# One expert with a fixed place, the others by their count, a ring in address order, and one branch around the rest

## The chip, the cores and the metric

The kernel runs on one core of a Trainium2 chip, in one launch. The metric is device time in microseconds (us), the median of three runs, and lower is better. The engines are PE (matrix multiply; PEld is its weight load), DVE (vector), ACT (scalar), POOL (GpSimd) and SP, which here issues weight loads. Each engine runs its own list of instructions in order; what one needs from another it waits for at a semaphore.

## The reference

Two transformer blocks run after each other on 512 tokens of width 1024, in float32. The change touches the last part alone, a mixture of experts: each token goes to 4 of 32 experts, and their results are added with gates. Cut to that:

```python
N_EXPERTS, TOP_K, D_MODEL, D_FF_EXPERT = 32, 4, 1024, 1024

def clamped_swiglu(hh):
    x_glu = jnp.minimum(hh[..., ::2], 7.0)
    x_lin = jnp.clip(hh[..., 1::2], -7.0, 7.0)
    return x_glu * jax.nn.sigmoid(1.702 * x_glu) * (x_lin + 1.0)

def moe_ffn(h, router_w, router_b, w1, b1, w2, b2):
    ht = h.reshape(t, d)                               # 512 x 1024
    logits = (ht @ router_w + router_b).astype(jnp.float32)
    top_val, top_idx = lax.top_k(logits, TOP_K)
    gates = jax.nn.softmax(top_val, axis=-1)
    ...                                                # tokens are sorted by expert, in blocks
    u = clamped_swiglu(h_pad[idx] @ w1[e] + b1[e])     # w1[e]: 1024 x 2048
    return u @ w2[e] + b2[e]                           # w2[e]: 1024 x 1024
    ...                                                # y[token] += gate * result

x = layer_norm(DEEPNORM_ALPHA * x + (1.0 + gt2) * ffn, ln2_g, ln2_b)
```

How many tokens an expert gets is known only once the router has run. Worked out with the reference on its own inputs, expert 1 gets 115 tokens, expert 0 gets 44, the next ones by size get 89, 87, 83 and 78; 15 of the experts 1 to 31 get more than 64 tokens, the other 16 get 64 or fewer.

## The kernel before

**Expert stage (`experts`).** The program has a fixed list of 32 places, j = 0 to 31. A place holds 2, 3 or 4 blocks of 32 tokens (`BLOCKS[j]`), so 64, 96 or 128 tokens. Places 0 and 1 belong to experts 0 and 1, with 3 blocks each. Which expert stands at each other place is found at run time: `places_of` counts the tokens of each expert, ranks the experts by count, and writes `order`, from which SP reads the expert's number (line 2140). Experts 0 and 1 are kept ahead by a constant that is added to their key (2 to the 20th). Of the others, ranks 2 and 3 get 4 blocks, ranks 4 to 17 get 3, ranks 18 to 31 get 2; `PLACES` puts a light one and a heavy one in turn, with the two of 4 blocks at j = 8 and 17. All blocks together: 84.

**One place.** `gather` (POOL, an indirect DMA from `hd`) fetches its token rows, `turned` transposes them on PE. `up` multiplies by w1 in 8 units of 128 rows (1 MB each), `swiglu` (DVE and ACT) makes u, `turn_u` transposes it, `down` multiplies by w2 in 4 units of 1 MB. Results are scaled by the gate (ACT) and added into the DRAM tensor `yd` by indirect DMAs from POOL (line 2310), one per block. On PE, `down` of a place stands behind `up` of the next; `slots` works out row numbers for two later places at a time.

**Weights.** Each unit is loaded by SP (`load`, line 1778) into a ring of `RING` = 13 buffers of 1 MB (tag `raw`); a load waits until PE has read what the buffer held 13 loads earlier. `tail` issues the first 13 loads ahead of the stage (`t.pre`): the 8 w1 units of expert 0 and 5 of expert 1. `up` takes from `pre`, `down` issues its own loads.

**The rest.** Tokens for which an expert's place has no room are dealt with after the 32 places. `rest` works out by how many tokens each expert is over, and the largest of these. If it is over 0 (line 2177), `make_lists` writes lists of those tokens, and a loop over all 32 experts (line 2179) runs four branches (line 2182), one for each 128 tokens, each around a copy of `more`: gather, up and down for one block list. Every pass of this loop begins with all engines meeting.

**The end (`final`).** SP loads `yd` in four parts (line 2358); DVE, ACT and POOL add, normalise and store tile by tile. It stands after the branch of line 2177.

Of the kernel before, what the change touches and what calls it, by code (L numbers as in the profile page):

```python
# [17 lines left out]
P = 128  # L18
S = 512
NT = S // P  # L20
NI = 2 * NT
D = 1024
KD = D // P
# [4 lines left out]
E = 32  # L28
TOPK = 4
LIMIT = 7.0  # L30
RING = 13


HEAVY, LIGHT = list(range(2, 18)), list(range(18, E))
PLACES = [0, 1] + [r for pair in zip(LIGHT, HEAVY[2:]) for r in pair]
PLACES[8:8], PLACES[17:17] = [2], [3]
BLOCKS = [4 if 2 <= r < 4 else 3 if r < 18 else 2 for r in PLACES]
LEVELS = (64, 32, 16, 8)
SWIGLU = 1.702

# [20 lines left out]
def constants():  # L61
    i = np.arange(P)
    c = {}
    c["ident"] = np.eye(P, dtype=np.float32)
    t, u = i[:, None], i[None, :]

    pairs = lambda s: ((t // s % 2 == 0) & (u // s == t // s + 1)).astype(np.float32)

    half = lambda m, s, j: m.reshape(P, 64 // s, 2, s)[:, :, j].reshape(P, 64)
    gm = [half(pairs(s), s, 1) for s in LEVELS]  # L70
    gm.append(((t // LEVELS[-1] == u // LEVELS[-1]) & (t <= u)).astype(np.float32))
    c["gmask"] = np.concatenate(gm, 1)
    bd = np.zeros((P, 256), np.float32)
    for h in range(4):
        bd[h * 32:(h + 1) * 32, h * 64:(h + 1) * 64] = 1.0
    c["bdiag"] = bd
    mm = np.zeros((P, 3, P), np.float32)
    mm[:, 0] = t <= u
    mm[:, 1] = t < u
    mm[:, 2] = t <= u  # L80
    c["mmask"] = mm
    xy = np.zeros((P, 4, 64), np.float32)
    for n, sz in enumerate((16, 32)):
        xy[:, 2 * n + 1] = half(pairs(sz), sz, 1)
        xy[:, 2 * n] = half(pairs(sz).T, sz, 0)
    c["xymask"] = xy
    c["dblk"] = np.ascontiguousarray((t // 16 == np.arange(8)[None, :]).astype(np.float32))
    c["eye16"] = np.broadcast_to(np.eye(16, dtype=np.float32).reshape(1, 256), (P, 256)).copy()
    tri = np.zeros((P, S), np.float32)
    tri[:, S - P:] = np.where(u <= t, 0.0, NEG)  # L90
    c["tri"] = tri
    hs = np.zeros((P, 2), np.float32)
    hs[:64, 0] = 1.0
    hs[64:, 1] = 1.0
    c["hsel"] = hs
    c["bd2"] = np.kron(np.eye(2), np.ones((64, 64))).astype(np.float32)

    e = np.arange(E)
    c["places"] = np.broadcast_to(np.stack([np.array(PLACES), 32 * np.array(BLOCKS), np.where(e < 2, 2.0 ** 20, 0) - e]),
                                  (P, 3, E)).astype(np.float32)  # L100
    c["group"] = (i[:, None] // 32).astype(np.float32)
    c["invf"] = np.broadcast_to((10000.0 ** (-np.arange(0, 32, 2, dtype=np.float64) / 32)).astype(np.float32), (P, 16)).copy()
    return c
# [1642 lines left out]
class Tail:  # L1746
# [27 lines left out]

    def load(self, part):

        w = self.k.t(self.k.rawp, [P, self.k.usize], tag="raw")
        self.k.nc.sync.dma_start(w if len(part.shape) == 2 else w.rearrange("p (h n) -> p h n", h=2), part)
        return w

# [340 lines left out]
    def experts(self, ctx):  # L2121
        k = self.k
        nc, I, tc = k.nc, k.I, k.tc
        self.prev = None
        self.mw = mw = k.pool("moew", 2, None, ctx, "right")
        xg = [k.t(mw, [P, D], tag="xg") for _ in range(2)]
        for x in xg:
            nc.gpsimd.memset(x, 0.0)
        xg = self.gather(self.idx[:, 0:1])
        self.biases(ctx)  # L2130
        x = self.turned(xg)
        self.slots(mw, [1])
        xg = self.gather(self.idx[:, 1:2])
        self.places_of(self.late)
        before = None
        for j in range(E):
            if j < 2:
                e, takes = j, k.ident[0:E, j:j + 1]
            else:
                e = nc.values_load(self.order[0:1, j:j + 1], engines=[mybir.EngineType.SP], min_val=0, max_val=E - 1)  # L2140
                takes = self.takes[:, j:j + 1]
            nxt = SimpleNamespace(nb=BLOCKS[j], rows=self.rows[:, j], gate=self.gate[:, j])
            one, nxt.two = self.weight(e)
            then = {}
            if j % 2 == 0 and j + 2 < E:
                then[0] = lambda: self.slots(mw, [j + 2, j + 3])
            if before is not None and before.uT is None:
                then[2] = lambda: self.turn_u(before)
            if j + 1 < E:
                def following():  # L2150
                    nonlocal x, xg
                    x = self.turned(xg)
                    if j + 2 < E:
                        xg = self.gather(self.idx[:, j + 2:j + 3])
                then[4] = following
            self.up(nxt, x, takes, one, then)
            if before is not None:
                self.down(before)
            if j == 0:
                self.turn_u(nxt)  # L2160
                self.down(nxt)
                nxt = None
            before = nxt
            with tc.issue_after(self.behind):
                if j in (2, 10):
                    self.last_rows(j // 8)
                if j == E - 1:
                    self.final_rows()
            if j in LB:
                with tc.issue_after(self.behind):  # L2170
                    self.last_bias(*divmod(LB.index(j), NT))
        self.turn_u(before)
        self.down(before)

        self.rest(self.late)
        most = nc.values_load(self.over[0:1, E:E + 1], min_val=0, max_val=S)
        with tc.If(most > 0):
            self.make_lists(mw)
            with tc.For_i(0, E, 1) as e:  # L2179
                n = nc.values_load(self.over[0:1, bass.ds(e, 1)], min_val=0, max_val=S)  # L2180
                for blk in range(NT):
                    with tc.If(n > P * blk):
                        self.more(e, blk)

    def more(self, e, blk):

# [101 lines left out]
    def down(self, st):  # L2288

        k = self.k  # L2290
        nc, tc = k.nc, k.tc
        mm = nc.tensor.matmul
        ps = [k.t(self.yp, [P, S], tag="y") for _ in range((st.nb + 1) // 2)]
        of = lambda b: ps[b // 2][:, b % 2 * 256:(b % 2 + 1) * 256]
        with tc.issue_after(self.prev):
            for c in range(4):
                w = self.load(st.two(c)).rearrange("p (h n) -> p h n", h=2)
                for h in range(2):
                    for b in range(st.nb):
                        for n in range(4):  # L2300
                            last = mm(of(b)[n * 32:(n + 1) * 32], st.uT[b][:, h, c * 32:(c + 1) * 32], w[:, h, n * 256:(n + 1) * 256],  # L2301
                                      start=c + h == 0 and b % 2 == 0,
                                      stop=c == 3 and h == 1 and (b % 2 == 1 or b == st.nb - 1))
        self.prev = last.ins
        yd = self.yd.rearrange("t (n c) -> (t n) c", n=4)
        done = []
        for b in range(st.nb):
            y = k.t(self.mw, [P, 256], tag="y", bufs=4)
            nc.scalar.activation(y, of(b), AF.Copy, scale=st.gate[:, b:b + 1])  # L2309
            s = nc.gpsimd.indirect_dma_start(out=yd, out_offset=bass.IndirectOffsetOnAxis(ap=st.rows[:, b:b + 1], axis=0),  # L2310
                                             in_=y, in_offset=None, bounds_check=4 * S - 1, oob_is_err=False, compute_op=OP.add)
            for o in done:
                tc.declare_no_dep(s.ins, o.ins, reason="each slot of an expert is another row")
            done.append(s)
# [34 lines left out]
    def final(self, out):  # L2349

        k = self.k
# [2 lines left out]
        H = [slice(n * S, (n + 1) * S) for n in range(2)]  # L2354
        ys = []
        for t in range(NT):
            ys.append(k.t(k.rawp, [P, k.usize], tag="raw")[:, :D])
            nc.sync.dma_start(ys[t], self.yd[t * P:(t + 1) * P])  # L2358
        tiny = k.t(self.mw, [P, NT, 4], tag="tiny", bufs=1)

# [23 lines left out]
def tail(k, t, out):  # L2384
    with ExitStack() as ctx:
        t.hp = k.pool("mmh", 4, PSUM, ctx)
        t.yp = k.pool("mmy", 2, PSUM, ctx)
        t.psp = k.pool("ps3", 2, PSUM, ctx)
        k.usize = 2 * D
        k.rawp = k.pool("rawx", RING, None, ctx, "left")  # L2390

        t.pre = [t.load(t.weight(i // KD)[0](i % KD)) for i in range(RING)]
        with ExitStack() as ec:
            t.experts(ec)
            t.final(out)
# [86 lines left out]
```

## Time and profile before

| | |
|---|---|
| median of 3 runs | 2831.96 us (2830.76 to 2844.21) |
| the profiled execution, its own time | 2832.56 us |
| its span, first to last instruction | 2830.8 us |
| PE busy | 1937.6 us, 68% of the span |
| DVE, ACT, POOL busy | 782.2, 492.8, 340.7 us |
| DMA | 539.66 MB, mean 191 GB/s |

The profile cuts the span into 40 slices of 70.8 us. A digit is the busy share of a slice in tenths; `PEclk` is the TensorE clock that was granted, in tenths of full speed; GB/s is what the DMA engines moved. The expert stage fills slices 13 to 28. A view "of a line" lists, beside the engines' work, what their sequencers did (PEldq, SPq): branches, register loads and waits, which are not counted as busy. In a timeline a row has start, duration, engine, line, operation, out<-in, and in brackets the idle time before it and what ended it. A view of waits has who waited for whom, us in total, times, and the longest.

### The profile page before, as it was taken

The page shows a single profiled execution, that of the slowest core. Times are in us where ns is not written, and L with a number is a line of the kernel's source. Part 1 is how long each engine was busy: PE and PEld are TensorE (multiplying, and loading weights), DVE is VectorE, ACT ScalarE, POOL GpSimd, SP SyncE. Part 2 cuts the span into 40 slices and gives each one's busy share as a digit, 9 for nine tenths or more (in the row PEclk, how much of TensorE's full clock was granted, in tenths as well). Part 3 has the DMA queues.
Part 4 walks back from the last instruction along what each step waited for, and adds up shares of the span by engine and source line. Part 5 has one row for each costly group of instructions (what it writes and reads, how often), then busy time and mean ns, then how long its engine had stood idle before and what let it go on. Part 6 is the DMA issues. An engine that isn't in the chain of part 4 may idle for free. (4 is left out here: it accounts for less than half of the span.)

```text
span 2830.8 us, 46626 instructions
## 1 busy us (share of the span) xinstructions
PE 1937.6 (68%) x17498; PEld 1129.8 (40%) x17499; DVE 782.2 (28%) x1915; ACT 492.8 (17%) x1089; POOL 340.7 (12%) x301
## 2 busy tenths in 40 slices
PE   7999998999987999999999999999240000000000
PEld 6787877788864343343334333433110000000000
DVE  6467375765763211211111111111010000000002
ACT  4143343344321111011111111111000000000000
POOL 0000103100232221031111111111200000000000
PEclk9899999999987999999999999999675555555555
DMA  6174155110236899989999999997400000000001
GB/s 223 38 221 147 57 167 185 38 37 16 72 123 278 318 409 407 388 316 408 410 411 383 393 404 394 395 404 274 179 13 6 6 6 6 6 6 6 6 6 64
DMA packets 150572, 539.66 MB, mean 191 GB/s; under 512 B 31789, under 2 KB 74333, under 8 KB 99248
## 3 DMA queue, kind: packets, MB, share of 16 engines
q1 hardware_dynamic: 123760, 500.63, 45.5%
q0 software_dynamic: 18368, 18.48, 3.0%
q10 hardware_dynamic: 7968, 13.20, 1.4%
q8 instruction: 422, 6.91, 1.3%
q14 instruction: 54, 0.44, 0.0%
HBM read 518.85 MB, written 25.36 MB: 192 GB/s over the span
## 5 line engine op out<-in xcount | busy, mean ns | idle before, releaser
L2244 PE MATMUL h<-raw,x 128*32 128x512 f32 x5632 | 660.9, 600 | 1.1 <-issue 1.1
L2244 PEld LDWEIGHTS h<-raw,x 128*32 128x32 f32 x5632 | 173.6, 110 | 396.3 <-issue 383.0
L2301 PE MATMUL y<-raw,uT 128*32 128x256 f32 x5632 | 315.6, 382 | 1.0 <-ACT uT L2286 0.8
L2262 DVE TENSOR_TENSOR h<-h,bias 128x512 f32<-128x512 f32 x88 | 60.5, 687 | 690.2 <-PE h L2244 690.2
L2301 PEld LDWEIGHTS y<-raw,uT 128*32 128x32 f32 x5632 | 182.9, 111 | 138.7 <-issue 21.2
L2310 POOL DMA_INDIRECT yd<-y,rows x84 | 132.0, 1571 | 677.2 <-ACT y L2309 632.3
L2364 DVE TENSOR_TENSOR raw<-raw,gt 128x512 f32<-128x512 f32 x4 | 2.7, 687 | 735.7 <-DMA raw<-yd 735.7
L2367 ACT ACTIVATE raw<-ar,tiny 128x1024 f32<-128x1024 f32 x4 | 4.6, 1151 | 733.6 <-DMA raw<-yd 722.9
L153 PE MATMUL mm<-hh,hi 128*128 128x512 f32 (+1 forms) x248 | 101.7, 410 | 0.0
L154 PE MATMUL mm<-hl,hi 128*128 128x512 f32 (+1 forms) x248 | 97.8, 395 | 0.0
L155 PE MATMUL mm<-hh,lo 128*128 128x512 f32 (+1 forms) x248 | 97.0, 393 | 0.0
L154 PE MATMUL mm<-lo,hh 128*128 128x384 f32 (+4 forms) x288 | 95.1, 330 | 2.0 <-DVE lo L148 2.0
L153 PE MATMUL mm<-hi,hh 128*128 128x384 f32 (+4 forms) x288 | 96.2, 336 | 0.4 <-ACT hh L205 0.4
L155 PE MATMUL mm<-hi,hl 128*128 128x384 f32 (+4 forms) x288 | 95.4, 332 | 0.0
L160 POOL TENSOR_TENSOR tiny<-tiny,mhalf 128x1 f32<-128x1 f32 x4 | 6.2, 1562 | 727.4 <-DMA raw<-yd 719.0
L147 ACT CAST hi<-raw 128x1024 fp32r<-128x1024 f32 (+5 forms) x77 | 66.3, 865 | 129.3 <-PE mm L154 65.3
L148 DVE TENSOR_TENSOR lo<-raw,hi 128x1024 fp32r<-128x1024 f32 (+5 forms) x77 | 76.8, 1001 | 32.3 <-ACT hi L147 30.3
L2270 ACT ACTIVATE sth<-sg 128x256 f32<-128x256 f32 x88 | 36.8, 418 | 254.0 <-DVE sg L2268 254.0
L2309 ACT ACTIVATE y<-y,gate 128x256 f32<-128x256 f32 x84 | 34.4, 472 | 201.5 <-PE y L2301 201.4
L2223 ACT COPY x<-ps 128x512 f32<-128x512 f32 x66 | 36.3, 589 | 152.0 <-PE ps L2222 146.8
L2251 ACT COPY bias<-ps 128x512 f32<-128x512 f32 x33 | 19.4, 587 | 249.4 <-PE ps L2249 249.4
L153 PEld LDWEIGHTS mm<-hi,hh 128*128 128x128 f32 x288 | 57.8, 201 | 7.0 <-issue 4.8
(706 smaller groups left out, 2911.9 us busy)
## 6 DMA issues: line engine op xcount, KB each, us to landing
raw<-in_exp_w SPq DMA_DIRECT2D x396, 1024.0 KB
mraw<-in_ada_w SPq DMA_DIRECT2D x48, 512.0 KB
raw<-in_w_in SPq DMA_DIRECT2D x30, 512.0 KB
raw<-in_w_in SPq DMA_DIRECT2D x16, 384.0 KB
raw<-in_w_out SPq DMA_DIRECT2D x8, 512.0 KB
raw<-in_w_o SPq DMA_DIRECT2D x16, 256.0 KB
yd<-x SPq DMA_DIRECT2D x5, 512.0 KB
x<-in_x SPq DMA_DIRECT2D x4, 512.0 KB
```

The lines of the kernel that those rows point to most:

```text
L147: nc.scalar.copy(hi, r)
L148: nc.vector.tensor_sub(lo, r, hi)
L153: mm(out, ah, bh, start=first, stop=False)
L154: mm(out, ah, bl, start=False, stop=False)
L155: return mm(out, al, bh, start=False, stop=last)
L2223: k.nc.scalar.copy(x[:, i * 4:i * 4 + 4], ps.rearrange("p (a n) -> p a n", a=4))
L2244: last = mm(ps[b][c * 32:(c + 1) * 32], x[:, i, b * 32:(b + 1) * 32], w[:, c * S:(c + 1) * S], start=i == 0, stop=i == KD - 1)
L2262: nc.vector.tensor_add(h, ps, bias)
L2270: nc.scalar.activation(th, g, AF.Tanh, scale=0.5 * SWIGLU)
L2301: last = mm(of(b)[n * 32:(n + 1) * 32], st.uT[b][:, h, c * 32:(c + 1) * 32], w[:, h, n * 256:(n + 1) * 256], start=c + h == 0 and b % 2 == ...
L2309: nc.scalar.activation(y, of(b), AF.Copy, scale=st.gate[:, b:b + 1])
L2310: s = nc.gpsimd.indirect_dma_start(out=yd, out_offset=bass.IndirectOffsetOnAxis(ap=st.rows[:, b:b + 1], axis=0), in_=y, in_offset=None, bo ...
```

## The change

1. `PLACES`, `BLOCKS` and the constant: only expert 0 keeps a fixed place (j = 0, 3 blocks). Experts 1 to 31 are ranked by count: rank 1 gets 4 blocks and stands at j = 17, ranks 2 to 16 get 3, ranks 17 to 31 get 2, light and heavy in turn from j = 1. All blocks together: 82.
2. `load` gives each buffer of the ring a tag of its own, `raw0` to `raw12`, taken in turn.
3. `tail` loads ahead the 8 w1 and the 4 w2 units of expert 0 (12, not 13); `down` takes from `pre` too. Expert 1's number is now read from `order` as any other.
4. `places_of` stands ahead of `slots` and of the gather for place 1.
5. In the loop of the rest a branch around all four (n > 0) holds the first `more` and, inside it, the other three branches.

```diff
-HEAVY, LIGHT = list(range(2, 18)), list(range(18, E))
-PLACES = [0, 1] + [r for pair in zip(LIGHT, HEAVY[2:]) for r in pair]
-PLACES[8:8], PLACES[17:17] = [2], [3]
-BLOCKS = [4 if 2 <= r < 4 else 3 if r < 18 else 2 for r in PLACES]
+PLACES = [0] + [r for pair in zip(range(17, E), range(2, 17)) for r in pair]
+PLACES[17:17] = [1]
+BLOCKS = [4 if r == 1 else 3 if r < 17 else 2 for r in PLACES]
...
-        w = self.k.t(self.k.rawp, [P, self.k.usize], tag="raw")
+        self.loads += 1
+        w = self.k.t(self.k.rawp, [P, self.k.usize], tag=f"raw{self.loads % RING}", bufs=1)
...
+        self.places_of(self.late)
         self.slots(mw, [1])
         xg = self.gather(self.idx[:, 1:2])
-        self.places_of(self.late)
...
-            if j < 2:
-                e, takes = j, k.ident[0:E, j:j + 1]
+            if j == 0:
+                e, takes = 0, k.ident[0:E, 0:1]
...
-                for blk in range(NT):
-                    with tc.If(n > P * blk):
-                        self.more(e, blk)
+                with tc.If(n > 0):
+                    self.more(e, 0)
+                    for blk in range(1, NT):
+                        with tc.If(n > P * blk):
+                            self.more(e, blk)
...
-                w = self.load(st.two(c)).rearrange("p (h n) -> p h n", h=2)
+                w = (self.pre.pop(0) if self.pre else self.load(st.two(c))).rearrange("p (h n) -> p h n", h=2)
...
-        t.pre = [t.load(t.weight(i // KD)[0](i % KD)) for i in range(RING)]
+        t.loads = -1
+        one, two = t.weight(0)
+        t.pre = [t.load(one(i)) for i in range(KD)] + [t.load(two(i)) for i in range(4)]
```

What SP issues at the start of the expert stage, before; `in_exp_w` are units of w1 and w2, `order` is the list of experts by place, an ISA row sets an address from a register:

```order
L1778 DMA raw_7821<-in_exp_w 128x2048
L1778 DMA raw_7823<-in_exp_w 128x2048
L1778 DMA raw_8144<-in_exp_w 128x2048
L1778 DMA raw_8170<-in_exp_w 128x2048
L1778 DMA raw_8196<-in_exp_w 128x2048
L1778 DMA raw_8222<-in_exp_w 128x2048
L1778 DMA raw_8343<-in_exp_w 128x2048
L1778 DMA raw_8357<-in_exp_w 128x2048
L1778 DMA raw_8378<-in_exp_w 128x2048
L2140 TENSOR_LOAD order_7909
L2140 ISA x2
L1778 ISA
```

The same place now:

```order
L1778 DMA raw_1748_7817<-in_exp_w 128x2048
L1778 DMA raw_1749_7819<-in_exp_w 128x2048
L1778 DMA raw_1750_7821<-in_exp_w 128x2048
L2140 TENSOR_LOAD order_7871
L2140 ISA x2
L1778 ISA
L1778 DMA raw_1820_8265<-in_exp_w 128x2048
L1778 ISA
L1778 DMA raw_1821_8275<-in_exp_w 128x2048
```

SP's first read of `order` stood behind 20 loads and stands behind 12; the loads of the second place follow it.

What PE does between the transposes of the first place's tokens (line 2222, now 2224) and its first matmuls of `up` (line 2244, now 2246), before; line 1941 picks tokens for `slots`, 2016 spreads row numbers, 2029 counts, 2046 makes `order`:

```order
L2222 MATMUL ps_7848<-ident_58,xg_7832 128x128 x4
L1941 MATMUL ps_7854<-val_4800,pick_7855 128x3 x4
L2244 MATMUL h_7936<-raw_7799,x_7841 32x512
L2016 MATMUL ps_7867<-f_1762_7862,ident_58 32x2 x16
L2029 MATMUL ps_7892<-tot_7890,ones_68 128x32
L2244 MATMUL h_7936<-raw_7799,x_7841 32x512 x3
L2244 MATMUL h_7937<-raw_7799,x_7841 32x512 x4
L2244 MATMUL h_7938<-raw_7799,x_7841 32x512
L2046 MATMUL ps_7907<-takes_7905,slot_4802 1x32
```

And now:

```order
L2224 MATMUL ps_7846<-ident_58,xg_7830 128x128 x4
L2029 MATMUL ps_7854<-tot_7852,ones_68 128x32
L2246 MATMUL h_7934<-raw_1739_7799,x_7839 32x512
L2046 MATMUL ps_7869<-takes_7867,slot_4802 1x32
L2055 MATMUL ps_7875<-ident_58,ge_4798 32x128 x4
L2055 MATMUL ps_7881<-ident_58,pm_4817 32x128 x4
L2246 MATMUL h_7934<-raw_1739_7799,x_7839 32x512 x3
```

The count and the order stand ahead of the picks for place 1, which follow some ten rows later.

PE at the end of the first of the four blocks of the rest, before; 2301 (now 2303) is a matmul of `down`:

```order
L2301 MATMUL y_17951<-raw_18054,uT_17948 32x256 x8
L2182 UNCONDITIONAL_BRANCH x2
L2182 COMPARE_AND_BRANCH
L2016 MATMUL ps_18118<-f_3275_18113,ident_58 32x2 x16
L2222 MATMUL ps_18142<-ident_58,xg_18137 128x128 x4
L2222 MATMUL ps_18148<-ident_58,xg_18137 128x128 x4
```

And now:

```order
L2303 MATMUL y_17791<-raw_3251_17894,uT_17788 32x256 x8
L2184 COMPARE_AND_BRANCH
L2016 MATMUL ps_17958<-f_3258_17953,ident_58 32x2 x16
L2224 MATMUL ps_17982<-ident_58,xg_17977 128x128 x4
L2224 MATMUL ps_17988<-ident_58,xg_17977 128x128 x4
L2246 MATMUL h_17994<-raw_3270_17998,x_17981 32x512 x4
```

The second branch was reached whatever the first decided; now it stands inside the first block's branch, whose jump passes all four blocks.

## Rows read from the trace of the kernel before

**Rows 1.** The page, part 2: 40 slices of the span

```profile
PE   7999998999987999999999999999240000000000
PEclk9899999999987999999999999999675555555555
GB/s 223 38 221 147 57 167 185 38 37 16 72 123 278 318 409 407 388 316 408 410 411 383 393 404 394 395 404 274 179 13 6 6 6 6 6 6 6 6 6 64
```

**Rows 2.** The page, part 5: swiglu's additions and the adds into `yd`, by count

```profile
L2262 DVE TENSOR_TENSOR h<-h,bias 128x512 f32<-128x512 f32 x88 | 60.5, 687 | 690.2 <-PE h L2244 690.2
L2310 POOL DMA_INDIRECT yd<-y,rows x84 | 132.0, 1571 | 677.2 <-ACT y L2309 632.3
```

**Rows 3.** Timeline, 1976 us to the end

```profile
1980.53 1.55 POOL L2310 DMA_INDIRECT yd<-y,rows  x1 [7.27 <-ACT y L2309]
...
1984.24 1.55 POOL L2310 DMA_INDIRECT yd<-y,rows  x1 [0.30 <-issue]
...
2021.34 0.36 SPq L2191 DMA_DIRECT2D slots<-lists  x1
...
2090.12 1.54 POOL L2310 DMA_INDIRECT yd<-y,rowsb  x1 [0.30 <-issue]
2800.03 6.07 SPq L2358 DMA_DIRECT2D raw<-yd  x4
2804.99 0.69 DVE L2364 TENSOR_TENSOR raw<-raw,gt 128x512 f32<-128x512 f32 x1 [735.74 <-DMA raw<-yd]
```

**Rows 4.** Of line 2180, 2100 us to the end: min/median/max ns, first and last start

```profile
L2180 PEldq TENSOR_LOAD <-overi x30: 301/306/317, 2101.2 to 2780.5; - x30
```

**Rows 5.** Of line 2182, 2100 to 2799 us: branches of the loop, same columns

```profile
L2182 DVEq COMPARE_BRANCH  x120: 116/116/124, 2101.5 to 2782.1; - x120
...
L2182 PEldq COMPARE_BRANCH  x120: 447/4584/5095, 2101.6 to 2794.5; - x120
```

**Rows 6.** Of line 2177, the branch around the rest, same columns as rows 4

```profile
L2177 SPq COMPARE_BRANCH  x1: 53/53/53, 1967.2 to 1967.2; - x1
...
L2177 PEldq COMPARE_BRANCH  x1: 100/100/100, 1979.3 to 1979.3; - x1
...
L2177 POOLq COMPARE_BRANCH  x1: 53/53/53, 1982.0 to 1982.0; - x1
```

**Rows 7.** Of the tile `yd`, 1950 us to the end: issue to landing

```profile
DMA to landing us min/median/max: 3.7/5.4/6.9
```

**Rows 8.** Stretches: us, busy of PE, PEld, DVE, ACT, POOL; PEclk, DMA share, GB/s

```profile
1180.00:1260.00 80.00, 80.00 (x972) 33.34 (x968) 12.88 (x37) 11.14 (x24) 22.77 (x17) 1.00 0.84 308
1260.00:1500.00 240.00, 235.94 (x2620) 92.99 (x2616) 45.63 (x121) 31.83 (x71) 38.80 (x28) 1.00 1.02 410
```

**Rows 9.** PE's waits, 940 to 1979 us: the only one for a weight load

```profile
PE y L2301 <- DMA raw<-in_exp_w: 0.3, 1, 0.3
```

**Rows 10.** PE's groups by shape, 990 to 1960 us: xcount | busy us, mean ns | idle before

```profile
L2244 PE MATMUL h<-raw,x 128*32 128x512 f32 x4864 | 568.5, 598 | 1.1 <-issue 1.1
L2301 PE MATMUL y<-raw,uT 128*32 128x256 f32 x4740 | 261.3, 379 | 0.0
...
L2283 PE MATMUL ps<-ident,u 128*128 128x128 f32 x150 | 23.0, 285 | 0.0
```

**Rows 11.** DMA, 990 to 1920 us

```profile
DMA packets 62892, 366.34 MB, mean 394 GB/s; under 512 B 10770, under 2 KB 18058, under 8 KB 20078
```

**Rows 12.** Timelines of POOL, PE and DVE at the start of the expert stage

```profile
875.43 1.10 POOL L2210 DMA_INDIRECT xg<-hd,idx  x1 [1.60 <-DVE tot L2027]
...
883.49 1.97 PE L2222 MATMUL ps<-ident,xg 128*128 128x128 f32 x8 [8.03 <-DMA xg<-hd,idx]
...
893.74 0.18 DVE L2048 TENSOR_SCALAR order<-ps 1x32 int32<-1x32 f32 x1 [1.75 <-PE ps L2046]
...
908.17 1.09 PE L2222 MATMUL ps<-ident,xg 128*128 128x128 f32 x8
```

**Rows 13.** Of line 1778, weight loads by SP, 870 to 1970 us, columns as rows 4

```profile
L1778 SPq DMA_DIRECT2D raw<-in_exp_w x382: 279/333/1088, 876.0 to 1956.7; - x191
```

More of the change, by code (lines that the diff above doesn't have):

```diff
@@ L98, in constants @@
     e = np.arange(E)
-    c["places"] = np.broadcast_to(np.stack([np.array(PLACES), 32 * np.array(BLOCKS), np.where(e < 2, 2.0 ** 20, 0) - e]),
+    c["places"] = np.broadcast_to(np.stack([np.array(PLACES), 32 * np.array(BLOCKS), np.where(e == 0, 2.0 ** 20, 0) - e]),
                                   (P, 3, E)).astype(np.float32)
@@ L2356, in final @@
         for t in range(NT):
-            ys.append(k.t(k.rawp, [P, k.usize], tag="raw")[:, :D])
+            ys.append(k.t(k.rawp, [P, k.usize], tag=f"raw{t}", bufs=1)[:, :D])
             nc.sync.dma_start(ys[t], self.yd[t * P:(t + 1) * P])
```

## The prediction

> **What bounds the kernel now.** Read the 40 slices of the page first [rows 1]. PE is nearly full up to slice 28; behind that lie ten slices in which no engine works, the DMA moves 6 GB/s, and only the last slice moves data again. That is a quarter of the span, and the share of busy time says nothing about it. Next come the counts [rows 2] and the timeline of that stretch [rows 3]. `swiglu` ran on 88 blocks and the 32 places hold 84, so the loop of the rest did work for one expert alone, one block list of 4 blocks. Its list was fetched at 2021.3 us, its last add into `yd` was issued at 2090.1, and SP loaded `yd` at 2800.0: 710 us later, with DVE idle for 735.7 us until the data came. So the end of the kernel waits for a loop that has no more work.
>
> What the loop does meanwhile is told by the lines of its register load [rows 4] and its branches [rows 5]. From 2101.2 us on there are 30 more passes, one per expert behind the one with work; with 32 passes in all, that one is the second, expert 1. A pass takes (2780.5 - 2101.2) / 29 = 23.4 us. In each, four branches jump over their blocks: 116 ns each on DVE, but 4584 ns (median) on PE, 18.3 of the 23.4 us. Every pass begins with all engines meeting, so all go at PE's pace.
>
> From PE's outer branch at 1979.3 us [rows 6] to the load of `yd` the rest takes 820.7 us: 42 before the list's fetch, 79.9 for the pass with work, 699 for the 30 empty ones. Ahead of it stands the expert stage, from the first transposes at 883.5 us [rows 12] to 1979.3, 1,096 us: PE is busy for 235.9 of 240 us beside a DMA at 410 GB/s, and for 80 of 80 where the DMA does 308 [rows 8]. In 1,039 us of it PE's matmuls wait for a load of weights once, for 0.3 us [rows 9]. PE bounds that stage.
>
> **The rest is not entered (change 1).** It was entered because expert 1's 115 tokens stood in a place of 96. Now expert 1 is ranked; it is the largest and gets rank 1 with 128. Whether another goes over follows from the ranks: ranks 4 to 16 and 18 to 31 keep their room and had enough, as only one expert was over. Less room have the old rank 2 and 3 (128, now 96; they need 89 and 87) and the old rank 17 (96, now 64; 15 experts need more than 64, and ranks 1 to 16 have room for 16 of them). Expert 0's 44 fit in 96. Those counts are from the reference's router on its own inputs, and they agree with the trace: one expert over, and it is expert 1. Then the largest excess is 0, the branch of line 2177 jumps, and the 820.7 us are replaced by what `final` needs from the last place.
>
> That is the last add into `yd`, issued at 1984.24 us [rows 3]. Adds land 3.7 to 6.9 us after issue, median 5.4 [rows 7]; I take the median: 1989.6. Then comes the join behind the jump, which the trace does not show. Below it is bounded by 0, above by one jump of PE, 4.6 us, paid by an engine that `final` needs. I take 2, nearer to the low end: SP and POOL reach the branch at 1967.2 and 1982.0 [rows 6] and PE at 1979.3, so that even jumps of 4.6 us are over before 1989.6; what is left are waits and semaphore updates. The load of `yd` would start at 1991.6 instead of 2800.0, 808.4 us sooner.
>
> [...]
>
> **Two blocks fewer in the stage (change 1).** 84 blocks become 82. One block is 64 matmuls of `up`, 64 of `down` and two transposes on PE [rows 10]: 64 x 568.5 / 4864 = 7.5 us, 64 x 261.3 / 4740 = 3.5, 2 x 23.0 / 150 = 0.3; 11.3 in all, 22.6 for two. The groups of these rows overlap by a per cent or two, so I take 22. It comes off the path only while PE stays the bound. A light place and a heavy one together need 25.2 MB, at 410 GB/s 61 us; PE, at the stage's own pace, needs 1096 / 84 x 5 = 65 for their 5 blocks. The ring of 13 buffers evens out a pair. So 22 off, bounds 0 and 26.
>
> **The start of the stage (changes 3 and 4).** `places_of` now stands ahead of `slots` and of the second gather; on PE the picks for place 1 move behind some 20 rows. The first gather took from 875.4 to 883.5 us [rows 12]; the second needs the new order, so by my estimate it is issued 2 to 3 us behind it, at about 896, lands 8 us later, at 904, and is needed at 908.2, so it stays hidden; were it not, PE would lose up to 5 us. SP must now have `order` for its 13th load, where it needed it for the 21st; behind that read stand the loads of place 1. `order` is there by 893.7 [rows 12] or a little sooner. The stream of loads starts at 876.0 [rows 13], and 12 of them at 410 GB/s take 30.7 us, so there is work for the DMA until then. No change on PE: 0, bounds -2 and +5.
>
> **Tags of the ring, one branch in the loop (changes 2 and 5).** Order and reach of the ring stay: load n waits for the reader of load n - 13, and 32 x 12 loads are the same 403 MB. Other addresses may free the first buffers sooner, but PE starts on its gathered tokens, not on weights, so nothing is gained. The inner branch is not reached when the rest is not entered. Both: 0.
>
> **The sum.** The load of `yd` moves from 2800.0 to 1991.6 - 22 = 1969.6 us. From there to the end nothing changes: 2830.8 - 2800.0 = 30.8. Span 2000.4, and with the 1.8 us between the profiled execution's time and its span 2002. That execution lies 0.6 us from the median, so I forecast **2002 us**.
>
> **The rivals.**
> *The loads set the stage's pace.* The DMA does 410 GB/s for long stretches [rows 8], as much as it does anywhere; were that the bound, two blocks fewer would give nothing: 2024 us. Against it: the mean is 394 GB/s [rows 11], 308 where PE is fully busy, and PE does not wait for loads.
> *An expert is still over* (a count on the chip differs, or the ranks do not do what I read). Then the loop runs with three jumps fewer per pass, 3 x 4.58 = 13.7 us: 31 x 13.7 = 425 off, 2832.6 - 22 - 425 = 2386. At most three more experts can be over, each for 79.9 - 9.7 = 70 us, so even that stays under the time before.
> *Slower: the ring loses its reach.* With a tag per buffer a load would wait not for its own buffer's reader but until the place before is done. Then each place pays its loads (12.6 MB, 30.7 us) on top of PE's 34 (1096 / 32), up to 32 x 30.7 = 980 us: 2980. It ends slower than before if more than 830 / 32 = 26 of the 30.7 us per place are exposed. For it: buffers, tags and waits are what the change rewrites. Against: SP's waits there name the same kinds, and 13 tags taken in turn are the same ring.
>
> **How the numbers follow.** Forecast 0.86, loads as the bound 0.06, an expert still over 0.05, the ring 0.02, and 0.01 for a gain that something eats up whole. Faster by over 0.5% (14 us, about what a measurement here tells from no change): 0.86 + 0.06 + 0.05 = 0.97; within 0.5% 0.01; slower 0.02. Range: down from 2002 by 4 (blocks), 4 (landing and join) and 2 (start), 1992, and 2 for what a profile leaves open: 1990. Up to the first rival, 2024, and 2 for the join: 2026. A slow join or a late gather without it, 2002 + 2.6 + 1.5 + 5 = 2011, lies inside.
>
> **What would show it.** Right: 82 blocks of `swiglu` and of adds, no instruction of `make_lists` or `more`, no empty slices, the load of `yd` 5 to 10 us after the last add's issue, and a stage some 20 us shorter with PE full. Wrong: register loads of line 2180 (an expert over); PE waiting for weight loads for tens of us (the rivals of loads and ring); PE idle near 905 us (gather); more than 7 us between the last add's landing and the load of `yd` (join).

## The result, and the profile of the changed kernel

The changed kernel takes 2016.8 us (median of 4 runs, 2009.1 to 2027.7); the kernel before took 2838.1 us beside it (4 runs, 2830.8 to 2847.1). The ratio is 0.711, 95% interval 0.707 to 0.715. Ratios, here and below, leave out executions over 1.5% above the fastest of their kernel. The forecast was 2002 us in a range of 1990 to 2026, the gain forecast 830 us, the measured one 821.

The page's 40 slices, which answer to [rows 1] (now about 50 us each):

```profile
PE   6999999989999999859999999999999999999992
PEclk9779896998999999869999999999999999999996
GB/s 261 63 29 249 146 167 26 136 131 224 61 41 26 12 12 115 219 186 291 284 406 411 409 412 356 407 415 407 413 413 389 405 398 407 397 394 403 407 277 147
```

The ten empty slices are gone: PE is nearly full to the last slice but one. The counts of part 5 (as in [rows 2]) are 82 and 82, so no block ran outside the 32 places:

```profile
L2264 DVE TENSOR_TENSOR h<-h,bias 128x512 f32<-128x512 f32 x82 | 56.3, 686 | 683.0 <-PE h L2246 683.0
L2312 POOL DMA_INDIRECT yd<-y,rows x82 | 128.8, 1571 | 658.1 <-ACT y L2311 642.8
```

The timeline of the end, which answers to [rows 3]:

```profile
1979.83 1.55 POOL L2312 DMA_INDIRECT yd<-y,rows  x1 [7.08 <-ACT y L2311]
1981.68 1.55 POOL L2312 DMA_INDIRECT yd<-y,rows  x1 [0.30 <-issue]
1983.54 1.55 POOL L2312 DMA_INDIRECT yd<-y,rows  x1 [0.30 <-issue]
1987.80 1.76 SPq L2360 DMA_DIRECT2D raw<-yd  x4
1992.01 0.69 DVE L2366 TENSOR_TENSOR raw<-raw,gt 128x512 f32<-128x512 f32 x1 [25.97 <-DMA raw<-yd]
```

From the last add's issue to the load of `yd` it is 4.3 us (1987.80 - 1983.54) where it was 815.8 (2800.03 - 1984.24 in [rows 3]): 811.5 us of the gain lie here, and DVE's idle time ahead of its first product fell from 735.7 to 26.0 us. The branch around the rest, with the columns of [rows 6], and what follows it on the other engines:

```profile
L2177 SPq EVENT_SEMAPHORE  x9: 17/17/17, 1972.0 to 1976.4; - x9
...
L2177 DVEq EVENT_SEMAPHORE  x2: 21/21/21, 1967.3 to 1967.4; - x2
L2177 ACTq EVENT_SEMAPHORE  x2: 17/17/17, 1980.6 to 1980.7; - x2
...
L2177 SPq COMPARE_BRANCH  x1: 53/53/53, 1966.7 to 1966.7; - x1
L2177 DVEq COMPARE_BRANCH  x1: 72/72/72, 1966.7 to 1966.7; - x1
L2177 PEldq COMPARE_BRANCH  x1: 3949/3949/3949, 1978.6 to 1978.6; - x1
L2177 ACTq COMPARE_BRANCH  x1: 54/54/54, 1980.1 to 1980.1; - x1
...
L2177 POOLq INC_SWDGE_SEM  x1: 836/836/836, 1986.8 to 1986.8; - x1
```

PE's one jump over the whole rest takes 3.9 us, and SP's first instruction behind its own jump comes 5.3 us after the branch; both are over before POOL is done with its adds, so nobody waits for them. DVE and ACT go on 0.6 and 0.5 us after their branches.

The expert stage runs from the first transposes to the last add:

```profile
901.46 1.97 PE L2224 MATMUL ps<-ident,xg 128*128 128x128 f32 x8 [9.08 <-DMA xg<-hd,idx]
```

That is 1082.1 us (1983.54 - 901.46), before 1100.8 (1984.24 in [rows 3] less 883.49 in [rows 12]). But it begins 18 us later than before.

### The profile page after: what moved, and what is told of

The parts are those of the page before. It is cut to its first block, busy times and chain, and to the rows that moved or that the text cites. A ratio compares the mean times of both kernels' runs of the same rounds, so it can differ in the third digit from the quotient of the medians.

```text
span 2017.8 us, 39725 instructions
## 1 busy us (share of the span) xinstructions
PE 1888.4 (94%) x16670; PEld 1112.0 (55%) x16671; DVE 770.5 (38%) x1861; ACT 483.5 (24%) x1070; POOL 312.9 (16%) x275
## 5 line engine op out<-in xcount | busy, mean ns | idle before, releaser
L2246 PE MATMUL h<-raw,x 128*32 128x512 f32 x5248 | 615.9, 598 | 0.0
L2246 PEld LDWEIGHTS h<-raw,x 128*32 128x32 f32 x5248 | 158.9, 110 | 365.2 <-issue 350.7
L2264 DVE TENSOR_TENSOR h<-h,bias 128x512 f32<-128x512 f32 x82 | 56.3, 686 | 683.0 <-PE h L2246 683.0
L2303 PE MATMUL y<-raw,uT 128*32 128x256 f32 x5248 | 291.8, 381 | 1.1 <-ACT uT L2288 1.1
L2303 PEld LDWEIGHTS y<-raw,uT 128*32 128x32 f32 x5248 | 169.9, 110 | 129.2 <-issue 17.3
L2251 PE MATMUL ps<-b,takes 32*32 32x512 f32 x248 | 63.8, 599 | 3.1 <-ACT x L2225 3.1
L926 DVE SCALAR_TENSOR_TENSOR acc<-mraw,cact,acc 128x1024 f32<-128x1024 f32 x42 | 53.7, 1279 | 20.5 <-DMA mraw<-in_ada_w 20.4
L153 PEld LDWEIGHTS mm<-lo,hh 128*128 128x128 f32 x288 | 57.9, 201 | 3.1 <-DVE lo L147 2.3
```

The source lines that it names most:

```text
L153: mm(out, ah, bl, start=False, stop=False)
L926: nc.vector.scalar_tensor_tensor(out=self.acc, in0=raw, scalar=self.act[:, kk:kk + 1], in1=self.acc, op0=OP.mult, op1=OP.add)
L2246: last = mm(ps[b][c * 32:(c + 1) * 32], x[:, i, b * 32:(b + 1) * 32], w[:, c * S:(c + 1) * S], start=i == 0, stop=i == KD - 1)
L2251: mm(pb[c * 32:(c + 1) * 32], takes.to_broadcast([E, 32]), self.b1[:, c * S:(c + 1) * S], start=True, stop=True)
L2264: nc.vector.tensor_add(h, ps, bias)
```

## The experiments

**Is the gain the rest that is not entered?** Two kernels put room for expert 1 into the kernel before and leave its order, its ring and its start as they were. The first:

```
-BLOCKS = [4 if 2 <= r < 4 else 3 if r < 18 else 2 for r in PLACES]
+BLOCKS = [4 if 1 <= r < 3 else 3 if r < 18 else 2 for r in PLACES]
```

> The kernel before with one number changed: of the two places with 4 blocks one is now place 1, which holds expert 1, and the old rank 3 gets 3 blocks; 84 blocks as before, old order, old ring, old start. Theory (the gain is that no expert is over, the two blocks are worth about 19 us, start and ring nothing): 2017 + 19 = 2036 us, ratio to the changed kernel 1.009. Rival A (the new order, ring or start earn part of the gain): later than 2045. Rival B (blocks are hidden behind loads): 2017.

Measured: ratio 0.999 (0.995 to 1.003) to the kernel before; the rest was entered and did 4 blocks, as before. The expectation missed how rooms are credited: by rank, and of the two fixed experts expert 1 has more tokens and so rank 0, whose room is place 0's. Place 1 got 4 blocks, the plan still gave expert 1 only 96 (19 of its tokens are computed twice here). So 4 blocks in another place are worth nothing by themselves. The second gives both fixed places 4 blocks:

```
+BLOCKS = [4 if r < 2 else 3 if r < 18 else 2 for r in PLACES]
```

> The kernel before with 4 blocks for places 0 and 1 and 3 for the old ranks 2 and 3: 84 blocks as before, old order, old ring, old start. Both fixed places get room, since the kernel credits rooms by rank among the two fixed experts, and expert 1 with more tokens is rank 0: with 4 blocks for place 1 alone the room went to expert 0. Theory (all of the 808 us is the rest that is not entered): time before minus 808, about 2022 us, ratio 0.715; against the changed kernel's stage the two blocks are left. Rival (new order, ring or start carry part of the gain): above 2045.

Measured: 2032.1 us, ratio 0.716 (0.711 to 0.721), 805 us less than before, where the theory had 808. One line of the kernel before carries 805 of the 821 us; the order, the ring and the start are not needed for it.

**What is a pass of the empty loop made of?** Change 5 alone, in the kernel before:

```
-for blk in range(NT):
-    with tc.If(n > P * blk):
-        self.more(e, blk)
+with tc.If(n > 0):
+    self.more(e, 0)
+    for blk in range(1, NT):
+        with tc.If(n > P * blk):
+            self.more(e, blk)
```

> The kernel before with change 5 alone: one branch around the four blocks of an expert, so an empty pass has one taken jump on PE instead of four. Theory (a far jump of PE costs 4.58 us whatever it jumps over, and all engines go at PE's pace): 31 passes lose 3 x 4.58 = 13.7 us each, 425 us in all, a pass of 9.7 us instead of 23.4, time about 2838 - 425 = 2413 us. Rival A (a jump costs 0.1 us and the 23.4 us of a pass are the meeting of the engines and the register loads): 31 x 3 x 0.1 = 9 us less, 2829. Rival B (a jump's price grows with what it jumps over; one jump over 1,200 PE instructions then costs what four over 300 do): no change, 2838.

Measured: 2250.8 us beside 2821.5 (one run each), 571 us less where 425 were expected. PE's rows of that branch and of the loop's own (line 2179), columns as in [rows 5]:

```profile
L2181 PEldq COMPARE_BRANCH  x32: 80/220/3377, 1986.2 to 2214.5; - x32
...
L2179 PEldq COMPARE_BRANCH  x33: 85/226/2528, 1989.9 to 2216.5; - x33
```

A jump over 1,200 PE instructions costs 0.22 us, not 4.58, and a pass 3.8 us (median of PE's register loads, start to start). Both rivals fall, and so does the theory's price: a far jump is not dear as such. The DMA shows what is. First the empty passes of the kernel before, 2101 to 2799 us (packets and MB of the queue that loads instructions), then those of this kernel, 2110 to 2214 us:

```profile
DMA packets 269, 4.39 MB, mean 6 GB/s; under 512 B 0, under 2 KB 0, under 8 KB 0
## 3 DMA queue, kind: packets, MB, share of 16 engines
q8 instruction: 267, 4.37, 3.6%
```

```profile
DMA packets 0, 0.00 MB, mean 0 GB/s; under 512 B 0, under 2 KB 0, under 8 KB 0
```

The 6 GB/s of the empty slices of [rows 1] were instructions: 9 packets of 16 KB per pass (267 / 30, and 4.37 MB / 267). With one branch none is loaded in that time.

Three kernels then enter the rest where nobody is over (`most < 1` in place of `most > 0` in the changed kernel), so that 32 empty passes run and no body ever does. With the old four branches:

> The changed kernel with the rest entered although no expert is over, and the loop's old four branches: 32 empty passes. Theory (the rest is 42 us before its loop and 23.4 us per empty pass, all of it behind the last add into yd): 42 + 32 x 23.4 = 791 us on top of the changed kernel's 2017, 2808 us. Rival (part of the 820 us went to the one block list with work, or is hidden now): well under 2700 us.

Measured: 2748.5 us. From the last add to the load of `yd` 757.7 us, a pass of 23.4 us and 264 instruction packets in 2010 to 2700 us: as in the kernel before. The expected time was 60 us too late: 38 of these are the rest (753 us longer than the 4.3 of the changed kernel, where 791 were expected, mostly because its first pass lies inside the 42 us ahead of the loop, and these begin before the last add), 28 are a start of the stage at 873.0 us instead of 901.5 (below), and a stage that is 4 us longer goes the other way.

> As the kernel with 32 empty passes and four branches, but the body that is jumped over holds 28 PE instructions instead of 300 (it leaves out nearly all matmuls of an expert in the rest; none is over here, so none of it would have run). Theory (PE's 4.58 us are the distance: the target has to be fetched; where 28 instructions are passed a jump costs 0.1 us as on DVE): a pass is 23.4 - 4 x 4.5 = 5.4 us, the rest 42 + 32 x 5.4 = 215 us, time 2232. Rival (a taken branch of PE costs 4.58 us whatever the distance): 2808 as with the full body.

> As the kernel with 32 empty passes and four branches, but with 160 PE instructions in each body instead of 300 (the part behind the up matmuls is left out of the rest). Theory in two forms: price by a step, with 160 already too far: 4.58 us per jump, 2808 us; or a step that 160 does not reach: 2232 us. If the price grows with the distance: 4.58 x 160 / 300 = 2.4 us per jump, a pass of 14.9 us, 42 + 32 x 14.9 = 519, time 2536.

Measured: 2180.9 us with 28 PE instructions per body, 2776.7 us with 160. PE's branches of line 2182 with 300, 28 and 160 instructions:

```profile
L2182 PEldq COMPARE_BRANCH  x124: 3348/4604/5123, 1994.8 to 2711.1; - x124
```

```profile
L2182 PEldq COMPARE_BRANCH  x124: 209/218/226, 2008.3 to 2146.8; - x124
```

```profile
L2182 PEldq COMPARE_BRANCH  x127: 3344/4592/5126, 1990.2 to 2734.6; - x127
```

The price is a step: 4.6 us with 160 as with 300, 0.22 with 28; growth with the distance falls. A pass takes 4.6 us where its jumps are short, without an instruction packet from 2020 to 2140 us; with 160 it takes 23.4 us and loads 9 instruction packets (267 in 2025 to 2720 us), as with 300. Bodies of 160 are not short for the engine: each matmul of the program becomes two weight loads and two matmuls (the 4 of line 2224 stand as x8 in the timeline above, and the changed stage has 11978 of each in its row below), so that in the built programs bodies of 28, 160 and 300 are some 90, 610 and 1,140 instructions of PE. Since a jump over 1,200 is cheap when it is the only one, the number of far stretches per pass must count. Two branches around two blocks each:

> As the kernel with 32 empty passes, but with two branches per pass on PE's way, each around two blocks of the rest. With one branch a pass took 3.8 us without any instruction loads, with four 23.4 us with 9 instruction loads of 16 KB. Theory (PE keeps two stretches of its program, and a pass that needs a third loads all of them again): three taken branches at 4 to 4.6 us each, a pass of 14 to 16 us, 42 + 32 x 15 = 522, time about 2530. Rival (what counts is the distance or a larger store, and only the four far stretches overflow it): a pass of about 4 us, time about 2175.

Measured: 2182.0 us, a pass of 4.6 us, no instruction packet from 2035 to 2140 us:

```profile
L2182 PEldq COMPARE_BRANCH  x64: 218/221/5327, 1966.5 to 2146.8; - x64
```

The expected limit of two stretches, an assumption of the author's, falls. This loop, whose pass touches three far stretches of PE's program, ran without an instruction packet in that time; the one with five (four jumps and the way back) had 9 in every pass. Whether three or four is the most that runs without, and whether it is the number of stretches or their size that counts, was not tried.

**Start, ring and blocks.** The changed kernel again, with 84 blocks (`4 if 1 <= r < 4`), with 80 (`3 if 0 < r < 16`), and with the old tag of the ring:

> The changed kernel again, as the yardstick for the three others of this chip. Expected 2017 us, and the first transposes of the expert stage anywhere between 883 us (as before) and 902 us (as in its first profile): theory, that the 17 us by which they came later there are the granted clock of that run, 0.85 instead of 0.91 in the first 400 us, on the same PE instructions; then runs of all kernels scatter by such an amount. Rival, that the change delays the front: then every run of the changed kernel has them near 900 us, and none near 883.

> The changed kernel with 84 blocks instead of 82 (ranks 2 and 3 get 4 blocks too). Theory (PE bounds the stage): 2 x 11 = 22 us more by the sum of the rows, 19 us by what the stage lost between the two profiles: ratio to the changed kernel 1.009 to 1.011. Rival (loads set the pace): 1.000.

> The changed kernel with 80 blocks (place 0 and rank 16 get 2 blocks; still every expert fits: expert 0 has 44 tokens, rank 16 has 64). Theory (PE bounds the stage): 22 us less, about 1995, ratio 0.989. Rival (with 82 blocks the loads are already as slow as PE, so fewer blocks give nothing): 1.000. In between if PE begins to wait for weights in the light pairs: a pair needs 25.2 MB, 61 us at 410 GB/s, and PE for 4 blocks 52 us, but only the first and last places become lighter.

> The changed kernel without change 2: the weights' buffers come from one tag of 13 again. Theory (order and reach of the ring stay): the same time, 2006 to 2017 us, and 1082 to 1086 us from the first transposes to the last add as in three profiles of the changed stage. Rival (the address order buys an earlier start of the loads): a stage longer by over 3 us.

Measured, ratios to the kernel before beside them: 0.706 (0.701 to 0.710) again, 0.710 (0.707 to 0.714) with 84, 0.700 (0.695 to 0.705) with 80, 0.712 (0.708 to 0.716) with the old ring. Against the changed kernel no ratio is clear of the noise. Runs of one kernel scatter by 15 to 45 us, so the stage from first transposes to last add tells more (one trace each; the kernel with bodies of 160 is left out, since two of its last adds stand behind the loop):

| kernel | blocks | stage, us | stage starts, us | clock, 0 to 400 us |
|---|---|---|---|---|
| before | 84 | 1100.8 | 883.5 | 0.91 |
| before, one branch | 84 | 1104.4 | 885.5 | 0.91 |
| before, 4 blocks for place 1 | 84 | 1107.6 | 872.4 | 0.94 |
| before, room for expert 1 | 84 | 1104.9 | 897.5 | 0.88 |
| changed, 84 blocks | 84 | 1096.3 | 883.5 | 0.91 |
| changed | 82 | 1082.1 | 901.5 | 0.85 |
| changed, again | 82 | 1085.4 | 901.5 | 0.86 |
| changed, empty passes (four, short, two) | 82 | 1085.9, 1085.8, 1083.0 | 873.0, 891.2, 887.2 | 0.94, 0.88, 0.91 |
| changed, old ring | 82 | 1087.1 | 886.4 | 0.88 |
| changed, 80 blocks | 80 | 1078.3 | 882.0 | 0.91 |
| changed, half loads | 82 | 1037.6 | 878.7 | 0.92 |

The *start* goes with the granted clock of the first 400 us, not with the kernel: 901.5 us at 0.85 and 0.86 (904.7 at 0.86 with bodies of 160), 872 to 887 at 0.91 to 0.94; at 0.88 it lies between 886 and 898, so that clock is not all of it. The built programs of the kernel before and of the changed one have the same PE instructions in the same order up to the first transposes; the row of the kernel before, of the changed one, and of the one with four empty branches (us, busy of PE, PEld, DVE, ACT, POOL, then the granted clock):

```profile
0.00:400.00 400.00, 376.83 (x1905) 307.33 (x1907) 236.18 (x445) 147.31 (x278) 23.24 (x46) 0.91 0.45 144
```

```profile
0.00:400.00 400.00, 377.76 (x1813) 306.19 (x1814) 221.03 (x425) 136.28 (x261) 23.56 (x46) 0.85 0.43 134
```

```profile
0.00:400.00 400.00, 375.75 (x1939) 306.73 (x1941) 241.33 (x456) 149.35 (x283) 23.68 (x47) 0.94 0.46 145
```

In equal time, equally busy, PE did 1905, 1813 and 1939 matmuls. The rival that the change delays the front falls: the changed front also started the stage at 873.0. What makes an execution's clock lower there was not found.

The *ring's tags* show no worth: 1087.1 us is 2.7 above the mean of the five traces of the changed stage, which themselves lie between 1082.1 and 1085.9. The *blocks*: from 84 to 82 the stage lost 12 us (1096.3 to 1084.4, that mean), from 82 to 80 another 6, where PE's rows say 22 and 22. What ate into it is told by PE's busy time in the stage; with 84 blocks, in the changed kernel with 82, and with 80 (columns as in the rows above):

```profile
883.47:1979.78 1096.31, 1074.94 (x12238) 436.50 (x12238) 195.60 (x556) 149.40 (x331) 193.23 (x139) 0.99 0.96 378
```

```profile
901.46:1983.54 1082.08, 1059.98 (x11978) 424.46 (x11978) 195.04 (x546) 147.13 (x327) 190.20 (x136) 0.99 0.97 382
```

```profile
882.01:1960.33 1078.32, 1045.83 (x11718) 418.85 (x11718) 190.04 (x536) 145.01 (x321) 187.10 (x135) 0.99 0.98 384
```

From 84 to 82 PE is idle for as long as before (21.4 and 22.1 us): the gain was not lost to waiting, the busy time itself fell by only 15 us. From 82 to 80 the busy time falls by 14 us and 10 us of idle time come in (32.5). Most of them stand in the last place, which now has two blocks: there, from 1924 us on, PE waits for its weights (line, operand, us in all, times, longest):

```profile
PE h L2246 <- DMA raw<-in_exp_w: 4.8, 4, 1.5
PE y L2303 <- DMA raw<-in_exp_w: 2.7, 5, 0.7
```

Waits for weights that [rows 9] does not show stand on PEld. The kernel before has these:

```profile
PEld h L2244 <- DMA raw<-in_exp_w: 10.3, 22, 0.8
```

In the traces of the changed stage they add up to between 9.0 and 18.4 us, with 80 blocks to 17.5, so they do not tell the kernels apart. At 84 blocks the changed kernel's stage is 5 to 11 us shorter than the four with the old order; what in the change does that was not separated. How much loads matter at all was asked with half the bytes:

> The changed kernel with only half of the columns of each expert weight loaded, and each loaded half used twice by PE: the same matmuls, half the bytes of weights; the other half of the experts' weights is left out of the computation. Theory (PE bounds the stage): the stage stays at 1082 to 1086 us. Rival (the two blocks gave 11 us where the rows of PE said 22 because the loads are nearly as slow as PE and share the bound): the stage gets shorter by 10 us or more, down to PE's own pace.

Measured: a stage of 1037.6 us, 47 less, and 0.3 us of waits for weights on PEld. So the stage does not stay, as the theory had it. But the loads are not all of it: PE's idle time in the stage fell only from 22 to 14 us, and its busy time by 36. With other loads the built program interleaves PE's work otherwise. The four matmuls of a place that bring the bias (line 2251) are then one run, in the changed kernel often two. Two pieces of PE's timeline, the changed kernel first (each matmul of the program counts as two):

```profile
1317.26 1.04 PE L2251 MATMUL ps<-b,takes 32*32 32x512 f32 x2
1318.23 5.36 PE L2246 MATMUL h<-raw,x 128*32 128x512 f32 x48
1323.52 1.05 PE L2251 MATMUL ps<-b,takes 32*32 32x512 f32 x6
1324.50 2.78 PE L2246 MATMUL h<-raw,x 128*32 128x512 f32 x24
```

```profile
1287.14 1.06 PE L2254 MATMUL ps<-b,takes 32*32 32x512 f32 x8
1288.13 2.78 PE L2249 MATMUL h<-raw,x 128*32 128x512 f32 x24
```

A run of one bias matmul holds PE for 0.97 us (1317.26 to 1318.23), of three for 0.98, of all four for 0.99: each of these runs costs about 1 us, with one, three or four matmuls in it. The built programs have 56 such runs before, 62 in the changed kernel, 58 with 84 blocks, 62 with 80 and 32 with half the loads. So by this estimate the changed kernel pays some 6 us for 6 more runs than before (4 of them against its form with 84 blocks), and the kernel with half the loads saves about 30 by 30 fewer; this share and that of the waits were not separated by a run, and a kernel that keeps the four together was not tried.

Of the kernels that compute everything the one with 80 blocks has the lowest time: 1984.7 us beside 2000.7 for the changed one on the same chip (medians of the 5 and 4 executions that the ratios compare). The intervals of the ratios overlap; its stage is 6 us shorter, in one trace.

## Why the prediction was right, and where it was not

Against the forecast span of 2000.4 us the profiled execution has 2017.8: 18.0 from the start of the stage, 3.3 from the stage, -3.1 from the join, -0.8 behind it.

- *The rest is not entered, because expert 1 gets 128 rows:* right, by the counts of 82, and by the one-line kernel that took 805 us off. The forecast of 808.4 us had a load of `yd` at 7.4 us behind the last add; 4.3 were measured (the add landed after 2.9 us, then 1.3 until the load, most of it POOL's 0.84 us of semaphore work). That is also less than the 5 to 10 us that the prediction gave as a sign of being right. The bound of 4.6 us for a jump that someone waits for did not come into play.
- *Two blocks, 22 us:* the term that was too large. The stage lost 18.7 us between the two profiles and 12 for the blocks alone, give or take the 4 us by which traces of one stage differ. The sum by PE's rows took their order for granted: from 84 to 82 blocks PE's busy time fell by 15 us, and its idle time hardly changed. Part of the difference are, by the estimate above, 4 more runs of bias matmuls; the rest stays open. The prediction also read waits for weights on PE alone [rows 9]; on PEld they were 10.3 us already. By the same rows the rival of loads that set the pace was called unlikely; as a bound on the whole stage it falls, since 82 blocks did shorten it, but a part of it is true: with 80 blocks PE waits 7.5 us for weights in the last place, and half the bytes made the stage 47 us shorter, by loads and order together.
- *Start of the stage, ring, 0:* right for the stage (the gather of place 1 hidden, the old ring within 3 us). But the sum took the front of one execution as fixed; it varies by 32 us between the profiles here (872.42 to 904.68), mostly with the clock (0.94 and 0.86 in those two). That is the largest error of the sum, and the range had no term for it. That the time still lies inside is luck: the upper end of 2026 was set by the rival of the loads, and the slowest of the four executions, 2027.7, is above it.
- *The reading of the empty passes:* 4.58 us per jump and all at PE's pace was right as read, and fewer jumps were right as a remedy. The explanation as a price per jump was wrong: an inner branch would have left a pass at 9.7 us by the prediction's rival of an expert still over, and it leaves 3.8. That rival should have been priced some 150 to 180 us lower: 31 x 5.9 = 183 by the passes, and the kernel with that one branch gained 146 us more than the price foretold.
- *Jumps and instruction packets:* PE's jumps of 4.6 us stand where a pass visits five far stretches of its program, with 9 packets of 16 KB per pass (267 and 264 packets with bodies of 300, 267 with 160), and not where it visits two or three: 0.22 us, and no packet from 2110 to 2214 and from 2035 to 2140 us. No run here shows how much of its program PE holds. The one jump over the rest took 3.9 us on PE, but DVE and ACT went on after 0.6 and 0.5 us.

## What to carry to other kernels

Read the end of the span before the shares: a loop that does nothing in 31 of 32 passes cost a quarter of this kernel, and one line of a capacity plan, matched to the counts, removed it. Where such a loop must stay, put one branch around everything that is rarely needed, so that a pass stays in a few stretches of PE's program (3.8 us a pass here, where four branches made it 23.4). For a term worth under 1% read the stage by its own ends, since the front moved the total by more here (its end lay at 872 to 905 us, at granted clocks of 0.94 and 0.86); and price a change in PE's work not only by the time of each matmul: look at the order as well, where short matmuls may stand in more and smaller runs (about 1 us each here).

## What the hardware showed that was not expected

- A taken jump of PE cost 0.22 us over 28 instructions, and over 1,200 in a loop with one jump per pass; with four far jumps per pass it cost 4.6 us, with 9 instruction packets of 16 KB per pass: 23.4 us for a pass in all, against 3.8 with the one.
- The granted clock of the first 400 us was between 0.85 and 0.94 on the same PE instructions, and the stage behind it began between 872 and 905 us.
- A run of 32-row bias matmuls held PE for about 1 us (0.97 to 0.99), whether it had one, three or four.
